# Two fp32 decoder blocks on one core: square products in 512-column chunks to the end of the row, last K tiles by token tile, and matmuls of constants at the start

## The chip, the core and the metric

The kernel runs on one core of one Trainium2 chip. The metric is the device time of one execution in microseconds, the median of several runs. TensorE (PE) multiplies; VectorE (DVE) and ScalarE (ACT) do the rest of the arithmetic; GpSimd (POOL) makes masks; SyncE's queue (SP) issues the DMAs.

## The reference

256 tokens of width 2048 go through two blocks, all in fp32. What matters here are the products of a 256-row activation with a wide weight matrix:

```python
# first block
proj = x @ w_in + b_in                     # 2048 -> 5376: conv value, glu, gate; q, k, v; gate
y_conv = layer_norm(conv31(c_val * sigmoid(c_glu))) ...   # depthwise, 31 taps
y = concat([y_conv, y_attn]) @ w_out + b_out              # square: 2048 -> 2048
x = layer_norm(ALPHA * x + y)
# second block, two layers (i = 0, 1)
y = mixer(x) @ w_out_a   (or w_out_b)                     # square
x = layer_norm(ALPHA2 * x + y)
x = x + (p[i] @ w_ple[i]) * sigmoid(x @ w_gate[i])        # square
```

So there are five square products, `w_out`, `w_out_a_2`, `w_gate0`, `w_out_b_2` and `w_gate1`. The first, second and fourth each lead into a layer norm over all 2048 columns; `w_gate1` is the last product of the kernel, and its result is stored.

## The kernel before

**Products.** TensorE takes fp32 operands here in a reduced form (`F32R`), so every operand is split into a high and a low part, and a product is three matmuls: high x high, high x low, low x high. Weights arrive by DMA as `raw`; ScalarE rounds them to `whi` (L277) and VectorE subtracts to get `wlo` (L278). `granules` (L291) walks the K tiles of a chunk of columns in groups of 128x1024 weights: two K tiles of 512 columns or four of 256. It keeps two groups cast ahead and three loaded ahead, over four buffers each of `whi` and `wlo` and six of `raw`. After each group it steps the side work by `side.pump()` (heads of the attention, the convolution's taps, rows of a norm), queued on VectorE behind the `wlo` of that group.

**`gemm`** (L315) has the activations stationary and the weights moving, for a chunk of up to 512 columns: an accumulator of two banks, one for each token tile `tt`, and for each K tile three matmuls into either bank (L324 to L326). **`gemm_T`** (L329) has the weights stationary and gives a transposed result: for each K tile a matmul of 512 moving columns for each 128 columns of weights (L336) and one of 256 (L338). The pool `acc` has two accumulators of two banks, the pool `aux` four single banks, which serve transposes, attention and the channel mean. The first product, `gv0`, has 512 columns and takes both accumulators; `total` (L341) then adds the two halves with the bias.

**Square products** run in the chunks of `SPANS` (L73):

```python
SPANS = ((0, 512), (512, 512), (1024, 512), (1536, 256), (1792, 256))
```

For `w_out` the chunks `c0` to `c4` hold eight K tiles only, as the other eight are done before. After each chunk VectorE adds it to `z` (L765, L780) and takes the statistics (`ln.stat`, L434); after the last, products of the small PLE matrices run on TensorE (`Ple.chunk`, L716; ScalarE copies each token tile's result, L720) while `ln.apply` (L436) makes mean and root, scales `z` (L448), and transposes it (L383) into scaled, shifted and split activations (L454, L459, L460). After `w_gate` ScalarE takes the sigmoid (L801), VectorE multiplies and adds (L802, L803), and the rows are stored (L805) or transposed for the next product.

**The start.** `glu(0)` runs `gv0` with the loads of x (L474) and their split (L376, L377) as events between its groups. After `kv` two transposes of `v` (L731) go to TensorE, which takes its instructions in order; the order on each engine is fixed beforehand by the framework's scheduler from estimated times.

Of the kernel before, what the change touches and what calls it, by code (L numbers as in the profile page):

```python
# [20 lines left out]
P = 128  # L21
# [9 lines left out]
LOAD = 3  # L31
PRE = 3
CONV_RATE = (3, 3)
BIG = 1e30
THETA = 10000.0

# [32 lines left out]
    **_twos("cg1", CT + 512),  # L69
}  # L70
CHUNKS_1 = {key: (ranges, ALL) for key, ranges in CHUNKS_1.items()}

SPANS = ((0, 512), (512, 512), (1024, 512), (1536, 256), (1792, 256))  # L73
CHUNKS_O1 = {
    **{f"a{c}": (_c(512 * c, 512), HIGH) for c in range(4)},
    **{f"c{c}": (_c(s, n), LOW) for c, (s, n) in enumerate(SPANS)},
# [48 lines left out]
def _cols(ranges):  # L125
    return sum(n for _, n in ranges)
# [58 lines left out]
def tile_net(ctx: ExitStack, tc: tile.TileContext, t: dict, out: bass.AP):  # L185
# [37 lines left out]
    ones_mean = const.tile([P, P], F32, name="ones_mean")  # L223
    nc.vector.memset(ones_mean, 1.0 / 1024.0)


    mask1 = const.tile([P, 384], F32, name="mask1")
    nc.gpsimd.memset(mask1, 0.0)
# [86 lines left out]
    def gemm(stream, key, act, events=None):  # L315

        n = _cols(STREAMS[stream][key][0])
        both = acc.tile([P, 2, 512], F32, tag="acc", name=uid("acc"))
        ps = [both[:, tt, :] for tt in range(2)]
        for kt, first, last, wh, wl in granules(stream, key, events):  # L320
            for tt in range(2):
                ah, al = act(kt, slice(tt * P, (tt + 1) * P))
                o = ps[tt][:, :n]
                nc.tensor.matmul(o, ah, wh, start=first, stop=False)  # L324
                nc.tensor.matmul(o, ah, wl, start=False, stop=False)  # L325
                nc.tensor.matmul(o, al, wh, start=False, stop=last)  # L326
        return [p[:, :n] for p in ps]

    def gemm_T(stream, key, act, events=None):  # L329

        nf = _cols(STREAMS[stream][key][0]) // P
        ps = [acc.tile([P, 2, 2, S], F32, tag="acc", name=uid("acc")) for _ in range(nf // 2)]
        for kt, first, last, wh, wl in granules(stream, key, events):
            both, ah = act.both(kt), act(kt, slice(0, S))[0]
            for f in range(nf):
                nc.tensor.matmul(ps[f // 2][:, f % 2], wh[:, f * P:(f + 1) * P], both, start=first, stop=False)  # L336
            for f in range(nf):
                nc.tensor.matmul(ps[f // 2][:, f % 2, 0, :], wl[:, f * P:(f + 1) * P], ah, start=False, stop=last)  # L338
        return ps

    def total(out_, ps, bias=None, scale=1.0):  # L341

        t = short((P, 2, S))
        if bias is None:
            nc.scalar.activation(t, ps[:, :, 1, :], AF.Copy, scale=scale)  # L345
        else:
            for f in range(2):
                nc.scalar.activation(t[:, f, :], ps[:, f, 1, :], AF.Identity, bias=bias1[:, bias + f:bias + f + 1])
        out_ = t if out_ is None else out_
        if scale == 1.0:  # L350
            nc.vector.tensor_tensor(out_, ps[:, :, 0, :], t, ALU.add)  # L351
        else:
            nc.vector.scalar_tensor_tensor(out_, ps[:, :, 0, :], scale, t, ALU.mult, ALU.add)
        return out_
# [373 lines left out]
    glu(2)  # L728
    glu(3)
    projected("kv", kvT)  # L730
    pt = transposes([kvT[:, 1, tt * P:(tt + 1) * P] for tt in range(2)])  # L731
    nc.scalar.copy(v1, pt[:, :S].rearrange("p (k s) -> p k s", k=2))
    for j in range(2):
        for f, h in enumerate("xy"):
            projected(f"q{j}{h}", qT[j][:, 2 * f:2 * f + 2, :])
        for i in range(4 * j, 4 * j + 4):
            side.add(attn1(i), 1, "ab"[i % 2])
        sag = unit((P, 4, S))
        for f, h in enumerate("xy"):
            projected(f"ag{j}{h}", sag[:, 2 * f:2 * f + 2, :], AF.Silu)  # L740
        sagT[j] = sag
# [424 lines left out]
```

## Time and profile before

| | us |
|---|---|
| median of 3 runs | 1449.77 |
| lowest, highest | 1449.68, 1450.47 |
| the profiled execution's own time | 1450.28 |
| its span, first to last instruction | 1448.6 |
| TensorE busy | 1432.4 (99%) |
| VectorE busy | 1032.3 (71%) |
| ScalarE busy | 802.9 (55%) |

The profile is one execution. A busy TensorE is not TensorE at its peak, as matmuls overlap: what one costs is read from start to start. In a group of instructions "xN" counts them; "[1.67 <-DVE h L351]" says that the engine had been idle for 1.67 us until line 351 on VectorE released it.

### The profile page before, as it was taken

What the parts mean: (1) busy time and instruction counts of PE and PEld (TensorE: products, weight loads), DVE (VectorE), ACT (ScalarE), POOL (GpSimd) and SP (SyncE); (2) the same over time, 40 slices, a digit from 0 to 9 for tenths busy, and PEclk for the clock granted to TensorE, in tenths of its full rate; (3) what the DMA queues carried; (4) which work ended last, traced back from release to release, by engine and by line L of the source; (5) the groups of instructions that cost most, each with busy time, mean ns of one, the idle gap of its engine ahead of it and who ended that gap; (6) DMA issues with size and microseconds to landing.
All of it is one profiled execution on the core that took longest, in us unless ns stands there. A gap on an engine that the chain in (4) does not pass through costs nothing.

```text
span 1448.6 us, 21304 instructions
## 1 busy us (share of the span) xinstructions
PE 1432.4 (99%) x8076; PEld 1240.1 (86%) x8076; DVE 1032.3 (71%) x1588; ACT 802.9 (55%) x1199; POOL 23.1 (2%) x51
## 2 busy tenths in 40 slices
PE   7999999999999999999999999999999999999998
PEld 6888888888997888888898898888888888889888
DVE  6999989998679966766758655655555555575754
ACT  6445778475545556646544545655655656554442
POOL 0000000000000000000000000100100001000000
PEclk9999999999999999999999999999999999999999
DMA  9765445556375655454764555555555555586462
GB/s 300 273 202 176 153 139 173 186 186 230 92 238 160 204 162 173 148 186 152 260 201 148 184 178 187 162 176 188 169 179 175 175 176 167 185 266 218 128 219 75
DMA packets 79798, 266.01 MB, mean 184 GB/s; under 512 B 9408, under 2 KB 10048, under 8 KB 79696
## 3 DMA queue, kind: packets, MB, share of 16 engines
q1 hardware_dynamic: 79632, 264.63, 56.5%
q8 instruction: 63, 1.03, 0.3%
q14 instruction: 39, 0.32, 0.1%
q0 software_dynamic: 64, 0.03, 0.0%
HBM read 262.53 MB, written 2.10 MB: 183 GB/s over the span
## 4 chain that ended last, share of the span: by engine, by line
PE 93%; DVE 4%; DMA 1%; issue 1%; ACT 1%; DVEq 0%; SPq 0%
PE acc L336 31%; PE acc L338 15%; PE acc L324 14%; PE acc L326 14%; PE acc L325 14%; DVE wlo L278 1%; PE o L602 1%; PE pt L383 1%; PE pT L578 1%; PE o L603 0%; DVE u L448 0%; DVE u L509 0%; PE z L1044 0%; PE z L1062 0%; DMA raw<-in_w_in_a 0%
## 5 line engine op out<-in xcount | busy, mean ns | idle before, releaser
L278 DVE TENSOR_TENSOR wlo<-raw,whi 128x1024 fp32r<-128x1024 f32 (+3 forms) x475 | 563.2, 1190 | 309.0 <-ACT whi L277 304.6
L277 ACT CAST whi<-raw 128x1024 fp32r<-128x1024 f32 (+3 forms) x475 | 485.2, 1025 | 489.3 <-PE acc L336 220.4
L336 PE MATMUL acc<-u,whi 128*128 128x512 f32 x2016 | 637.2, 399 | 7.3 <-DVE u L377 5.6
L338 PEld LDWEIGHTS acc<-u,wlo 128*128 128x128 f32 x2016 | 377.0, 188 | 87.7
L338 PE MATMUL acc<-u,wlo 128*128 128x256 f32 x2016 | 394.9, 279 | 0.0
L324 PE MATMUL acc<-whi,u 128*128 128x512 f32 (+3 forms) x1004 | 359.0, 358 | 0.0
L325 PE MATMUL acc<-wlo,u 128*128 128x512 f32 (+3 forms) x1004 | 355.9, 354 | 0.8 <-DVE wlo L278 0.8
L326 PE MATMUL acc<-whi,u 128*128 128x512 f32 (+3 forms) x1004 | 355.6, 354 | 0.0
L336 PEld LDWEIGHTS acc<-u,whi 128*128 128x128 f32 x2016 | 309.3, 189 | 14.2 <-ACT whi L277 5.6
L326 PEld LDWEIGHTS acc<-whi,u 128*128 128x128 f32 x1004 | 189.7, 189 | 25.4 <-DVE u L377 0.4
L324 PEld LDWEIGHTS acc<-whi,u 128*128 128x128 f32 x1004 | 189.8, 189 | 25.0 <-issue 1.7
L325 PEld LDWEIGHTS acc<-wlo,u 128*128 128x128 f32 x1004 | 189.9, 189 | 24.3 <-DVE wlo L278 1.2
L509 DVE SCALAR_TENSOR_TENSOR u<-u,convw,u 128x255 f32<-128x255 f32 (+19 forms) x240 | 109.2, 465 | 3.9
L351 DVE TENSOR_TENSOR h<-acc,h 128x512 f32<-128x512 f32 x51 | 34.8, 684 | 4.8 <-ACT h L345 4.8
L376 ACT CAST u<-h 128x512 fp32r<-128x512 f32 (+1 forms) x32 | 18.0, 566 | 25.3 <-DVE h L615 17.5
L466 DVE TENSOR_TENSOR u<-u,h 128x1024 f32<-128x1024 f32 x24 | 28.5, 1219 | 3.4 <-DMA h<-in_ln_g 3.3
L377 DVE TENSOR_TENSOR u<-h,u 128x512 fp32r<-128x512 f32 (+1 forms) x32 | 19.7, 622 | 14.4 <-ACT u L376 14.1
L1034 POOL TENSOR_SCALAR_AFFINE_SELECT h<-h 128x256 f32<-128x256 f32 x32 | 18.1, 564 | 743.8 <-DVE h L1054 715.7
L558 ACT ACTIVATE u<-u,negm 128x128 f32<-128x128 f32 x64 | 28.4, 445 | 2.7 <-DVE negm L550 2.6
L345 ACT ACTIVATE h<-acc 128x512 f32<-128x512 f32 x42 | 24.9, 593 | 5.5 <-PE acc L338 4.0
L802 DVE TENSOR_TENSOR h<-h,u 128x512 f32<-128x512 f32 (+1 forms) x20 | 10.8, 582 | 20.8 <-ACT h L801 20.8
L277 ACT CAST u<-raw 128x1024 fp32r<-128x1024 f32 (+1 forms) x17 | 17.3, 1015 | 14.2 <-DMA raw<-in_w_ple 7.4
(197 smaller groups left out, 962.8 us busy)
## 6 DMA issues: line engine op xcount, KB each, us to landing
raw<-in_w_in_a SPq DMA_DIRECT2D x80, 512.0 KB, 3.6
raw<-in_w_in SPq DMA_DIRECT2D x76, 512.0 KB, 3.4
raw<-in_w_gate SPq DMA_DIRECT2D x64, 512.0 KB, 3.6
raw<-in_w_kv_b SPq DMA_DIRECT2D x64, 512.0 KB, 3.4
raw<-in_w_q_b SPq DMA_DIRECT2D x64, 512.0 KB, 3.3
raw<-in_w_out SPq DMA_DIRECT2D x32, 512.0 KB, 3.4
raw<-in_w_out_a SPq DMA_DIRECT2D x32, 512.0 KB, 4.3
raw<-in_w_out_b SPq DMA_DIRECT2D x32, 512.0 KB, 4.4
```

The costliest lines, as they stand in the source:

```text
L277: nc.scalar.copy(hi, raw)
L278: return hi, lo, nc.vector.tensor_tensor(lo, raw, hi.bitcast(F32), ALU.subtract)
L324: nc.tensor.matmul(o, ah, wh, start=first, stop=False)
L325: nc.tensor.matmul(o, ah, wl, start=False, stop=False)
L326: nc.tensor.matmul(o, al, wh, start=False, stop=last)
L336: nc.tensor.matmul(ps[f // 2][:, f % 2], wh[:, f * P:(f + 1) * P], both, start=first, stop=False)
L338: nc.tensor.matmul(ps[f // 2][:, f % 2, 0, :], wl[:, f * P:(f + 1) * P], ah, start=False, stop=last)
L345: nc.scalar.activation(t, ps[:, :, 1, :], AF.Copy, scale=scale)
L351: nc.vector.tensor_tensor(out_, ps[:, :, 0, :], t, ALU.add)
L466: nc.vector.tensor_tensor(self.z[c], self.z[c], r.unsqueeze(1).broadcast_to([P, 2, 512]), op)
L509: nc.vector.scalar_tensor_tensor(o[:, d:], h[:, :S - d], w, o[:, d:], ALU.mult, ALU.add)
L558: nc.scalar.activation(sc[:, i, cs], sc[:, i, cs], AF.Exp, bias=negm[:, i, tt:tt + 1], scale=-1.0, accum_out=den[:, i, tt:tt + 1],)
```

## The change

It does five things. `SPANS` becomes four chunks of 512 columns, for all five square products. `gemm` keeps back the K tiles of a chunk's last group and then issues them by token tile: all of token tile 0, then all of token tile 1. `gemm_T` gives `gv0`, its only product with four column tiles, one accumulator and two banks of `aux`, and `total` adds such a pair bank by bank. Nine fp32 matmuls of a constant with itself go to TensorE first. And the two transposes of `v` with the copy to `v1` move from behind `kv` to behind `q0x` and `q0y`.

```diff
--- before.py
+++ after.py
@@ -31,6 +31,7 @@
 LOAD = 3
 PRE = 3
 CONV_RATE = (3, 3)
+WARM = 9
 BIG = 1e30
 THETA = 10000.0
 
@@ -69,8 +70,7 @@
     **_twos("cg1", CT + 512),
 }
 CHUNKS_1 = {key: (ranges, ALL) for key, ranges in CHUNKS_1.items()}
-
-SPANS = ((0, 512), (512, 512), (1024, 512), (1536, 256), (1792, 256))
+SPANS = tuple((512 * c, 512) for c in range(4))
 CHUNKS_O1 = {
     **{f"a{c}": (_c(512 * c, 512), HIGH) for c in range(4)},
     **{f"c{c}": (_c(s, n), LOW) for c, (s, n) in enumerate(SPANS)},
@@ -223,6 +223,10 @@
     ones_mean = const.tile([P, P], F32, name="ones_mean")
     nc.vector.memset(ones_mean, 1.0 / 1024.0)
 
+    idle = bank("idle")
+    for i in range(WARM):
+        nc.tensor.matmul(idle[:, 0:P], ones_mean, ones_mean, start=True, stop=True)
+
 
     mask1 = const.tile([P, 384], F32, name="mask1")
     nc.gpsimd.memset(mask1, 0.0)
@@ -317,36 +321,57 @@
         n = _cols(STREAMS[stream][key][0])
         both = acc.tile([P, 2, 512], F32, tag="acc", name=uid("acc"))
         ps = [both[:, tt, :] for tt in range(2)]
+
+        def product(tt, kt, first, last, wh, wl):
+            ah, al = act(kt, slice(tt * P, (tt + 1) * P))
+            o = ps[tt][:, :n]
+            nc.tensor.matmul(o, ah, wh, start=first, stop=False)
+            nc.tensor.matmul(o, ah, wl, start=False, stop=False)
+            nc.tensor.matmul(o, al, wh, start=False, stop=last)
+
+        ends = STREAMS[stream][key][1][-_group(*STREAMS[stream][key]):]
+        late = []
+        for step in granules(stream, key, events):
+            late.append(step)
+            if step[0] in ends and not step[2]:
+                continue
+            for tt in range(2):
+                for one in late:
+                    product(tt, *one)
+            late = []
+        return [p[:, :n] for p in ps]
+
+    def gemm_T(stream, key, act, events=None):
+
+
+
+
+        nf = _cols(STREAMS[stream][key][0]) // P
+        two = acc.tile([P, 2, 2, S], F32, tag="acc", name=uid("acc"))
+        ps = [two[:, f] for f in range(2)]
+        ps += [bank("acc").rearrange("p (h s) -> p h s", h=2) for _ in range(2, nf)]
         for kt, first, last, wh, wl in granules(stream, key, events):
-            for tt in range(2):
-                ah, al = act(kt, slice(tt * P, (tt + 1) * P))
-                o = ps[tt][:, :n]
-                nc.tensor.matmul(o, ah, wh, start=first, stop=False)
-                nc.tensor.matmul(o, ah, wl, start=False, stop=False)
-                nc.tensor.matmul(o, al, wh, start=False, stop=last)
-        return [p[:, :n] for p in ps]
-
-    def gemm_T(stream, key, act, events=None):
-
-        nf = _cols(STREAMS[stream][key][0]) // P
-        ps = [acc.tile([P, 2, 2, S], F32, tag="acc", name=uid("acc")) for _ in range(nf // 2)]
-        for kt, first, last, wh, wl in granules(stream, key, events):
-            both, ah = act.both(kt), act(kt, slice(0, S))[0]
+            pair, ah = act.both(kt), act(kt, slice(0, S))[0]
             for f in range(nf):
-                nc.tensor.matmul(ps[f // 2][:, f % 2], wh[:, f * P:(f + 1) * P], both, start=first, stop=False)
+                nc.tensor.matmul(ps[f], wh[:, f * P:(f + 1) * P], pair, start=first, stop=False)
             for f in range(nf):
-                nc.tensor.matmul(ps[f // 2][:, f % 2, 0, :], wl[:, f * P:(f + 1) * P], ah, start=False, stop=last)
-        return ps
+                nc.tensor.matmul(ps[f][:, 0, :], wl[:, f * P:(f + 1) * P], ah, start=False, stop=last)
+        return [two, ps[2:]][:nf // 2]
 
     def total(out_, ps, bias=None, scale=1.0):
 
         t = short((P, 2, S))
+        out_ = t if out_ is None else out_
+        if isinstance(ps, list):
+            for f, p in enumerate(ps):
+                nc.scalar.activation(t[:, f, :], p[:, 1, :], AF.Identity, bias=bias1[:, bias + f:bias + f + 1])
+                nc.vector.tensor_tensor(out_[:, f, :], p[:, 0, :], t[:, f, :], ALU.add)
+            return out_
         if bias is None:
             nc.scalar.activation(t, ps[:, :, 1, :], AF.Copy, scale=scale)
         else:
             for f in range(2):
                 nc.scalar.activation(t[:, f, :], ps[:, f, 1, :], AF.Identity, bias=bias1[:, bias + f:bias + f + 1])
-        out_ = t if out_ is None else out_
         if scale == 1.0:
             nc.vector.tensor_tensor(out_, ps[:, :, 0, :], t, ALU.add)
         else:
@@ -728,11 +753,12 @@
     glu(2)
     glu(3)
     projected("kv", kvT)
-    pt = transposes([kvT[:, 1, tt * P:(tt + 1) * P] for tt in range(2)])
-    nc.scalar.copy(v1, pt[:, :S].rearrange("p (k s) -> p k s", k=2))
     for j in range(2):
         for f, h in enumerate("xy"):
             projected(f"q{j}{h}", qT[j][:, 2 * f:2 * f + 2, :])
+        if j == 0:
+            pt = transposes([kvT[:, 1, tt * P:(tt + 1) * P] for tt in range(2)])
+            nc.scalar.copy(v1, pt[:, :S].rearrange("p (k s) -> p k s", k=2))
         for i in range(4 * j, 4 * j + 4):
             side.add(attn1(i), 1, "ab"[i % 2])
         sag = unit((P, 4, S))
```

## Rows read from the trace of the kernel before

**Rows 1.** Page, part 4: chain that ended last, shares of the span by engine.

```profile
PE 93%; DVE 4%; DMA 1%; issue 1%; ACT 1%; DVEq 0%; SPq 0%
```

**Rows 2.** Waits of TensorE, whole run: total us, times, longest us.

```profile
PE acc L336 <- DVE h L351: 1.7, 1, 1.7
PE pt L383 <- DVE h L351: 1.6, 1, 1.6
```

**Rows 3.** Windows, TensorE alone: stretch, length, busy us (count), PEclk, DMA share, GB/s.

```profile
1316.86:1339.90 23.04, 23.04 (x194) 1.00 0.58 188
1339.90:1350.81 10.91, 10.91 (x50) 1.00 0.28 96
```

**Rows 4.** Timeline, 0-34 and 303 us: start, length, engine, line, operation, tiles, count.

```profile
5.59 2.04 PE L336 MATMUL acc<-u,whi 128*128 128x512 f32 x4 [5.59 <-DVE u L377]
...
10.80 1.09 PE L336 MATMUL acc<-u,whi 128*128 128x512 f32 x4
...
25.82 0.62 ACT L376 CAST u<-h 128x512 fp32r<-128x512 f32 x1 [2.05 <-DMA h<-in_xT]
...
26.47 0.69 DVE L377 TENSOR_TENSOR u<-h,u 128x512 fp32r<-128x512 f32 x1 [1.98 <-ACT u L376]
...
27.64 1.09 PE L336 MATMUL acc<-u,whi 128*128 128x512 f32 x4
...
27.95 3.67 DVE L278 TENSOR_TENSOR wlo<-raw,whi 128x1024 fp32r<-128x1024 f32 x3
...
29.97 0.63 PE L338 MATMUL acc<-u,wlo 128*128 128x256 f32 x4
...
32.27 0.73 PE L336 MATMUL acc<-u,whi 128*128 128x512 f32 x2 [1.67 <-DVE h L351]
...
303.00 0.70 PE L647 MATMUL cm<-u,ones_mean 128*128 128x256 f32 x2
```

**Rows 5.** Windows: length; busy us of PE, PEld, DVE, ACT, POOL; PEclk, DMA share.

```profile
15.00:20.00 5.00, 5.00 (x30) 4.33 (x29) 3.09 (x6) 2.89 (x6) 0.00 (x0) 1.00 1.00 320
...
40.00:60.00 20.00, 20.00 (x116) 17.45 (x116) 19.75 (x34) 9.48 (x12) 0.00 (x0) 1.00 0.78 273
```

**Rows 6.** Timeline, 113 to 116 us: around the transposes of `v`.

```profile
113.20 0.63 PE L336 MATMUL acc<-u,whi 128*128 128x512 f32 x2
...
114.65 0.68 DVE L351 TENSOR_TENSOR h<-acc,h 128x512 f32<-128x512 f32 x1
...
115.48 0.41 PE L383 MATMUL pt<-ident,h 128*128 128x128 f32 x2 [1.65 <-DVE h L351]
```

**Rows 7.** Timeline, 62 to 67 us: one group's low half and its first use.

```profile
62.92 1.22 DVE L278 TENSOR_TENSOR wlo<-raw,whi 128x1024 fp32r<-128x1024 f32 x1
...
66.29 0.40 PE L338 MATMUL acc<-u,wlo 128*128 128x256 f32 x2
```

**Rows 8.** Timeline, 763 to 770 us: end of `w_out_a_2`, VectorE and ScalarE.

```profile
763.94 0.76 DVE L780 SCALAR_TENSOR_TENSOR u<-u,acc 128x256 f32<-128x256 f32 x2 [0.58 <-PE acc L326]
...
766.68 1.08 ACT L720 COPY u<-acc 128x512 f32<-128x512 f32 x2 [1.69 <-PE acc L326]
...
769.40 1.07 ACT L720 COPY u<-acc 128x512 f32<-128x512 f32 x2 [1.22 <-PE acc L326]
```

**Rows 9.** Timeline, two chunks' ends of `w_gate1`; stores: count, KB, us to landing.

```profile
1420.47 1.09 ACT L801 ACTIVATE h<-acc 128x512 f32<-128x512 f32 x2 [1.67 <-PE acc L326]
...
1423.02 0.95 SPq L805 DMA_DIRECT2D out<-u  x2
...
1443.50 0.66 ACT L801 ACTIVATE h<-acc 128x256 f32<-128x256 f32 x2 [9.92 <-PE acc L326]
...
1445.04 0.81 SPq L805 DMA_DIRECT2D out<-u  x2
...
out<-u SPq DMA_DIRECT2D x6, 256.0 KB, 2.2
...
out<-u SPq DMA_DIRECT2D x4, 128.0 KB, 1.9
```

## Prediction, made before the changed kernel ran

> **What bounds the kernel now.** I read the chain of work that ended last first: TensorE holds 93% of it [rows 1], so a microsecond of TensorE work or of TensorE waiting is a microsecond of the kernel, apart from what lies after its last matmul. Then the table of who waited for whom, for TensorE: two long waits on VectorE besides the first one, 1.7 us in the product `g1` and 1.6 us in a transpose [rows 2]. Then the stretches in which only one kind of matmul runs, for the price of a matmul from start to start [rows 3]; the "mean ns of one" of a group is a latency and cannot be used, because matmuls overlap. Last, the timelines at the start, at 113 us, at the end of a square product and at the end of the kernel [rows 4, 6, 8, 9].
>
> **The change, part by part.**
>
> *Chunks of 512.* Each of the five square products ends in two chunks of 256 columns, now in one of 512. A 256-column matmul costs 23.04 us / 192 = 120.0 ns (the stretch counts 194 because it touches one on either side), a 512-column one 10.91 / 48 = 227.3 ns [rows 3]. So two halves cost 12.7 ns more than the whole: something of about 13 ns is paid per matmul, whatever its width. A chunk is 16 K tiles x 2 token tiles x 3 = 96 matmuls, 48 where the product has eight K tiles: 4 x 192 + 96 = 864 of 256 columns go, 432 of 512 take their place: 864 x 0.1200 - 432 x 0.2273 = 103.7 - 98.2 = **-5.5 us**, all on the path, since these stretches show TensorE busy without a gap. Weight loads, casts and groups of weights (128x1024 each, eight for the last 512 columns either way) keep their sizes and number. The Trainium skill, "TensorE: Matmul & The Clock Gate", section "Back-to-back issue gap", has 2.5 ns per matmul beside N/2.4: by that page the part would be worth 432 x 2.5 = 1.1 us (an estimate from the page), and the whole change 4.4 us less than below; the rows' 120.0 and 227.3 ns, against its 109 and 216, disagree with it, and the measurement decides.
>
> *Two more banks for `gv0`.* The first product has held both accumulator tiles, so `g1` could not start before VectorE had read one: TensorE's last matmul of `gv0` starts at 30.32 (the fourth of the 29.97 row), the next at 32.27 [rows 4]. With the other half of `gv0` in two auxiliary banks, `g1` has a free tile. Its first weights are there: the low halves of its first three groups, one of which lasts TensorE 2.8 us, are made from 27.95 to 31.62. Start to start 1.95 us less the 0.12 of one matmul: **-1.8 us**. The two added VectorE adds are half as wide; they cost VectorE some 0.15 us and TensorE nothing. The auxiliary banks are next asked for at 115 us [rows 6].
>
> *Transposes of `v` after `q0x`, `q0y`.* TensorE's row of matmuls stops at 113.43 (the second of the 113.20 row) and goes on with a transpose at 115.48, which waits for VectorE's total of `kv` at 114.65 [rows 6]. That total is late because VectorE is late, not TensorE. Behind 22 us of `q0` matmuls the total is long done: 2.04 - 0.23 = **-1.8 us**. What moves along is a bank and ScalarE's copy to `v1`, behind the casts and totals of `q0`; nothing on SP or POOL. `v1` is first used by a head's last matmuls, after its softmax, which itself comes after `q0`.
>
> *Nine warm-up matmuls.* TensorE is idle until 5.59 us [rows 4]. No row shows such a matmul at that hour. The nearest is the 256-column fp32 matmul of `channel_mean`, 0.70 us in work at full clock with its two records [rows 4]: nine of them are 6.3 us, would end at some 7.4 and hold up the first product by 1.8; from below the price is nothing. With half the columns, at half the clock, overlapping, I take 3 us, hidden in the idle time. What they may give: the first four wide matmuls take 2.04 us and later ones 1.09 [rows 4], the spacing of 1.2 and of 2.4 GHz. Two K tiles take from 5.59 to 10.80, the next twelve from there to 27.64, 1.40 each; at full clock the first two would save 5.21 - 2.80 = 2.4 us. But the product cannot end sooner than its data: the last pair of x tiles lands at 25.8, is split by 27.16, and its matmuls start at 27.64 [rows 4], while the DMA engines are busy throughout [rows 5]. So at most 27.64 - 27.16 = 0.48 arrives: **-0.4 us** (bounds 0 and -2.4, the latter if loads come sooner too).
>
> *Is VectorE able to follow?* From 40 to 60 us it is busy 19.75 of 20 us [rows 5], so its results come no sooner when TensorE does. The tightest group of weights has its low half done at 62.92 + 1.22 = 64.14 and is first used at 66.29 [rows 7]: 2.15 us of slack, against 1.8 + 0.4 = 2.2 gained before it. Here 0.0 to 0.3 us comes back: **+0.2 us**. I found no tighter group in the first 140 us.
>
> *Last K tiles by token tile.* Would token tile 0 be read sooner? The rows speak against it: VectorE's two adds after a chunk start together at 763.94, after 0.58 us of waiting, though token tile 0 was complete 0.36 us before the last matmul; ScalarE's copies at 766.68 likewise [rows 8]. Both token tiles lie in one tile of two banks, and the first reader waits for its last matmul. So **0**.
>
> *The longer end of a chunk.* With 512 columns in the last chunk and no earlier release, what follows gets longer. At the kernel's end a 512-column chunk takes from 1420.47 to the end of its second store's issue at 1423.97 = 3.50 us, a 256-column one from 1443.50 to 1445.85 = 2.35; stores of 256 KB take 0.3 us longer to land (2.2 against 1.9) [rows 9]: **+1.45 us**, all on the path, since TensorE is done. At the three norms adds and statistics take 0.8 to 1.5 us longer (up to twice 0.76 for each of the two pairs [rows 8]); there PLE matmuls run (24 x 0.2273 = 5.5 us, twice that at the last), and the first scaling on ScalarE stands behind the copies at 769.40 + 1.07 anyway [rows 8]. That hides it but for some 0.1 us each: **+0.25** (bounds 0 and 1.8).
>
> Sum: -5.5 - 1.8 - 1.8 - 0.4 + 0.2 + 1.45 + 0.25 = **-7.6 us**. Against the profiled execution's own 1450.28 that is 1442.7; that execution lies 0.5 above the median of the three runs, 1449.77, so I forecast **1442.2** for a median.
>
> **Rivals.**
>
> *Early release.* If the new program does let token tile 0 be read when its own six last matmuls are done, 1.36 us before the end, half of each pair of copies leaves the path (0.5 us at three norms [rows 8]), and the kernel's tail shrinks to about that of 256 columns (-1.15), and the +0.25 goes: -10.5, 1439.3. For it: the reorder makes the lead four times what it was. Against: the 0.58 us that VectorE waited. The Trainium skill, "PSUM — Partial Sum Buffer", section "Summary: rules for kernel authors", lets another bank be read while a matmul runs, so the chip would allow it; no run here shows it yet.
>
> *VectorE takes the front back.* If the order in VectorE's queue turns out worse than the slack above, TensorE waits for low halves of weights between 40 and 140 us, and the 1.8 + 1.8 + 0.4 come back less the 0.2 already counted: -7.6 + 3.8 = -3.8, 1446.0. For it: 19.75 of 20 us [rows 5]. Against: 2.15 us of slack in the tightest group [rows 7]. Counted with it, at 0.02 of its 0.13, is the case that a matmul's fixed price is not what the rows show: if only a fifth of the 12.7 ns went with each of the 432, 1.1 us of the 5.5 would be left, 1446.6. Against: both spacings held over 192 and 48 matmuls [rows 3]. (That fifth is about what the page named above gives.)
>
> *Slower.* The order on each engine is laid down beforehand from estimated times, and changes with every edit. A transpose placed before its data costs TensorE 1.8 us, as at 113 us. The transposes of 16 heads and the norm's 8 groups all wait for a VectorE that runs late. From 6 such stops on (6 x 1.8 = 10.8 > 7.6 + 2.9) the kernel is slower by over 0.2%; with 7, 1449.8 - 7.6 + 12.6 = 1454.8. Against: before, one such place, that of `v`, stalls for long.
>
> *The part doesn't act.* The warm-up may leave the clock as it was: 0.4 us, inside the range.
>
> **How the numbers follow.** Forecast 0.63, its own range 1440.2 (loads come sooner) to 1443.8 (the norms' tails show); early release 0.20; VectorE takes it back 0.13; slower 0.04. 1438.7 to 1444.8 holds the forecast, most of early release and little else, about 8 in 10. A measurement of this kernel tells 0.2%, 2.9 us, from no change: faster means below 1446.9. That holds for the first two cases and for most of the third (0.91 in all); 0.05 within; 0.04 slower.
>
> **What would show it.** Right: on the three lines of `gemm` 432 matmuls fewer and none of 256 columns; the last product's end some 9 us earlier than 1443.5; no wait of `g1` or of the `v` transposes; both adds after a chunk still starting together; a tail about 1.4 us longer. Wrong: matmuls of 512 columns spaced over 230 ns in the last chunk, waits on `wlo` in the first 140 us, the second reader of a chunk starting 1.36 us after the first, or new stops at transposes.

## The result, and the profile after

The changed kernel takes 1441.71 us, median of 6 runs (1440.68 to 1443.9), against 1449.72 of the kernel before (1448.77 to 1453.32): a ratio of 0.9942, 95% interval 0.993 to 0.9955, or 8.0 us less. The forecast was 1442.2 in a range of 1438.7 to 1444.8. The two profiled executions are further apart, 1450.28 and 1441.06, since one lies 0.6 above its median and the other 0.7 below. Their spans, 1448.58 and 1439.31, differ by 9.27 us, and that is what the table takes apart. A step is the change in the start of one stage of TensorE against the stage before it.

| part | forecast | profiles, after less before |
|---|---|---|
| wait of `g1` for an accumulator | -1.8 | -1.83 |
| rest of the first product (clock) | -0.4 | -0.21 |
| a low half of weights that comes late, at 72 us | +0.2 | +0.26 |
| transposes of `v` | -1.8 | -1.92 |
| five square products with their norms, to the last matmul | -5.5 + 0.25 | -5.87 |
| one stop at 462 us | not foreseen | -0.92 |
| from the last matmul to the end | +1.45 | +1.17 |
| other steps | | +0.05 |
| sum | -7.6 | -9.27 |

First the chain of waits of the changed kernel, as shares of the span. Before, VectorE held 4% of it [rows 1]; now TensorE has all but a few per cent.

```profile
PE 97%; DVE 1%; ACT 0%; DMA 0%; issue 0%; SPq 0%; DVEq 0%
```

The waits of TensorE (total, times, longest) answer [rows 2]: the two long ones are gone, and what is left stands at the start (L228 is the constant's first matmul, L402 splits x, L356 multiplies) and at the norms (L473 scales, L408 transposes).

```profile
PE acc L356 <- DVE u L402: 1.6, 4, 0.7
PE idle L228 <- DVE halfpi L878: 1.2, 1, 1.2
PE pt L408 <- DVE u L473: 0.5, 1, 0.5
PE pt L408 <- ACT h L479: 0.3, 1, 0.3
```

The timeline of TensorE at the places of [rows 4] and [rows 6]. The constant's matmuls run from 1.15 to 5.36 us and the first four wide matmuls take 1.17 instead of 2.04; at 9.54 TensorE waits for x, as it did not before. `g1` starts at 30.23, straight behind `gv0`. At 72.03 two wide matmuls are followed after 0.74 us, not 0.47. The transposes of `v`, at 130.94, wait for nothing.

```profile
1.15 4.21 PE L228 MATMUL idle<-ones_mean 128*128 128x128 f32 x18 [1.15 <-DVE halfpi L878]
5.78 1.17 PE L356 MATMUL acc<-u,whi 128*128 128x512 f32 x4 [0.42 <-DVE u L402]
...
9.54 1.21 PE L356 MATMUL acc<-u,whi 128*128 128x512 f32 x4 [0.73 <-DVE u L402]
...
29.75 0.64 PE L358 MATMUL acc<-u,wlo 128*128 128x256 f32 x4
30.23 0.63 PE L356 MATMUL acc<-u,whi 128*128 128x512 f32 x2
...
72.03 0.63 PE L356 MATMUL acc<-u,whi 128*128 128x512 f32 x2
72.77 0.51 PE L358 MATMUL acc<-u,wlo 128*128 128x256 f32 x2
...
130.94 0.38 PE L408 MATMUL pt<-ident,h 128*128 128x128 f32 x2
```

A window over the last product's last chunk, TensorE alone: 48 matmuls and one touched on either side in 10.91 us, as before in a chunk of 512 columns [rows 3].

```profile
1421.50:1432.41 10.91, 10.91 (x50) 1.00 0.00 0
```

Last, a chunk's end in `w_out_a_2` and the kernel's end, as in [rows 8, 9]. Both readers of an accumulator still stand in one row, and only the first of them waited for TensorE. The first sigmoid (L827) starts after the last matmul's end at 1433.02, and the second store's issue ends at 1436.54.

```profile
757.36 1.29 DVE L806 SCALAR_TENSOR_TENSOR u<-u,acc 128x512 f32<-128x512 f32 x2 [0.41 <-PE acc L330]
...
1433.06 1.08 ACT L827 ACTIVATE h<-acc 128x512 f32<-128x512 f32 x2 [9.82 <-PE acc L330]
1433.69 1.29 DVE L828 TENSOR_TENSOR h<-h,u 128x512 f32<-128x512 f32 x2 [9.20 <-ACT h L827]
1434.90 1.29 DVE L829 TENSOR_TENSOR u<-u,h 128x512 f32<-128x512 f32 x2
1435.61 0.93 SPq L831 DMA_DIRECT2D out<-u  x2
```

### The profile page after: what moved, and what is told of

Read it like the earlier page. It is cut to its first block, busy times and chain, and to the rows that moved or that the text cites. A ratio compares the mean times of both kernels' runs of the same rounds, so it can differ in the third digit from the quotient of the medians.

```text
span 1439.3 us, 20447 instructions
## 1 busy us (share of the span) xinstructions
PE 1429.0 (99%) x7662; PEld 1220.4 (85%) x7662; DVE 1029.5 (72%) x1569; ACT 803.6 (56%) x1195; POOL 23.1 (2%) x51
## 4 chain that ended last, share of the span: by engine, by line
PE 97%; DVE 1%; ACT 0%; DMA 0%; issue 0%; SPq 0%; DVEq 0%
PE acc L356 32%; PE acc L358 16%; PE acc L328 14%; PE acc L330 14%; PE acc L329 14%; PE pt L408 1%; PE o L627 1%; PE pT L603 1%; PE o L628 0%; PE z L1070 0%; PE z L1088 0%; PE s L570 0%; DMA h<-in_xT 0%; DVE wlo L282 0%; PE o L618 0%; PE s L568 0%
## 5 line engine op out<-in xcount | busy, mean ns | idle before, releaser
L282 DVE TENSOR_TENSOR wlo<-raw,whi 128x1024 fp32r<-128x1024 f32 (+3 forms) x475 | 563.6, 1191 | 314.0 <-ACT whi L281 309.5
L356 PE MATMUL acc<-u,whi 128*128 128x512 f32 x2016 | 636.5, 398 | 1.6 <-DVE u L402 1.6
L328 PE MATMUL acc<-whi,u 128*128 128x512 f32 (+2 forms) x860 | 334.1, 388 | 0.0
L329 PE MATMUL acc<-wlo,u 128*128 128x512 f32 (+2 forms) x860 | 330.6, 384 | 0.0
L330 PE MATMUL acc<-whi,u 128*128 128x512 f32 (+2 forms) x860 | 330.5, 384 | 0.0
L356 PEld LDWEIGHTS acc<-u,whi 128*128 128x128 f32 x2016 | 308.3, 189 | 9.1 <-issue 5.0
L330 PEld LDWEIGHTS acc<-whi,u 128*128 128x128 f32 x860 | 161.6, 188 | 30.8 <-DVE u L402 0.4
L328 PEld LDWEIGHTS acc<-whi,u 128*128 128x128 f32 x860 | 161.6, 188 | 30.5 <-issue 1.7
L329 PEld LDWEIGHTS acc<-wlo,u 128*128 128x128 f32 x860 | 161.8, 188 | 28.6 <-DVE wlo L282 0.2
L534 DVE SCALAR_TENSOR_TENSOR u<-u,convw,u 128x255 f32<-128x255 f32 (+22 forms) x240 | 108.0, 466 | 3.3
L401 ACT CAST u<-h 128x512 fp32r<-128x512 f32 (+1 forms) x32 | 18.0, 566 | 22.0 <-DVE h L640 18.8
L402 DVE TENSOR_TENSOR u<-h,u 128x512 fp32r<-128x512 f32 (+1 forms) x32 | 19.7, 622 | 10.2 <-ACT u L401 10.0
L828 DVE TENSOR_TENSOR h<-h,u 128x512 f32<-128x512 f32 x16 | 10.4, 689 | 19.1 <-ACT h L827 19.1
```

The source lines that it names most:

```text
L282: return hi, lo, nc.vector.tensor_tensor(lo, raw, hi.bitcast(F32), ALU.subtract)
L356: nc.tensor.matmul(ps[f], wh[:, f * P:(f + 1) * P], pair, start=first, stop=False)
L534: nc.vector.scalar_tensor_tensor(o[:, d:], h[:, :S - d], w, o[:, d:], ALU.mult, ALU.add)
```

## The experiments

The theory: the parts add up; the square products gain a fixed price per matmul; the order by token tile gives nothing because both token tiles lie in one tile; the clock gives next to nothing because x has to land. The rivals: the price per matmul is smaller, the order releases something, VectorE takes the front back. In the expectations "the page" with its 2.5 ns is the page of the Trainium skill that the prediction names for the price of a matmul. The runs come in four groups, each with runs of the kernel before beside it: the three single parts and "token tiles apart" in the first, where "before" was 1449.71; the four from "the kernel before once more" to "eight chunks" in the second, 1449.95; the version in turn, the four K tiles and the halves in the third, 1451.25; the last version in the fourth, 1451.17. So "before" itself moved by 1.5 us between groups, and where two versions come from different groups, a median proves no difference of a microsecond: there the stages of the profiles are compared.

### One part alone: the chunks

```diff
-SPANS = ((0, 512), (512, 512), (1024, 512), (1536, 256), (1792, 256))
+SPANS = tuple((512 * c, 512) for c in range(4))
```

> The kernel before with SPANS as four chunks of 512 columns and nothing else. Theory (a fixed price of some 12.7 ns per matmul): 432 pairs of 256-column matmuls become 432 of 512, -5.5 us up to the last product's end, +1.2 us of longer work behind the last matmul, so about -4 us (1445.5); last matmul's end about 5.5 us earlier than 1443.5. Rival (the page's 2.5 ns per matmul): -1.1 up to the last matmul, so about +0.1 in all. A second question: the 0.8 us for which TensorE waited on VectorE's low halves of weights near 462 us, and which is gone in the changed kernel. If it is gone here, the new chunks in the first square product reordered VectorE's queue there, and the run gives -5; if it stays, it belongs to one of the other parts.

Measured: 1445.33, -4.4 us, ratio 0.9971 (0.996 to 0.9982). The profiled execution, 1443.85, is the fastest of the seven, and that of before lies 0.6 above its median, so the two profiles differ by 6.5 us; what follows compares their stages. The last matmul ends 7.6 us earlier than before, at 1435.82, of which 0.9 is the stop at 462, which is gone here, and 0.7 lies before `w_out` (two stops that vary, see below). From the first matmul of `w_out` to the last of PLE behind it TensorE takes 93.67 us instead of 94.37, for `w_out_a_2` 94.69 instead of 95.99, for `w_gate0` 92.03 instead of 93.82, for `w_out_b_2` to `w_gate1` 191.37 instead of 194.05. The theory's matmuls alone make -0.61, -1.22, -1.22 and -2.44. The excess of 0.57 in `w_gate0` is two stops at transposes between the matmuls of its halves, which now stand behind the product: the next stretch is 0.51 longer. The other three exceed the theory by 0.08 to 0.24. A price of 2.5 ns would have left the time where it was; that rival falls.

### One part alone: the banks of `gv0`

```diff
-        ps = [acc.tile([P, 2, 2, S], F32, tag="acc", name=uid("acc")) for _ in range(nf // 2)]
+        two = acc.tile([P, 2, 2, S], F32, tag="acc", name=uid("acc"))
+        ps = [two[:, f] for f in range(2)]
+        ps += [bank("acc").rearrange("p (h s) -> p h s", h=2) for _ in range(2, nf)]
...
```

> The kernel before with the first product's second half in two auxiliary banks and nothing else. Theory: the first matmul of g1 follows the last of gv0 without the 1.67 us wait, -1.8 us at g1, and at most 0.3 us of it is given back between 40 and 140 us: -1.6 us (1448.1). Rival (VectorE takes the front back): g1 starts 1.8 us sooner, but the start of w_out is no more than 0.3 us sooner. The wait near 462 us is here as before, unless a shift of the front by 1.8 us alone removes it.

Measured: 1446.41, -3.3 us, ratio 0.9978 (0.9969 to 0.9987); twice what was expected. The wait of `g1` is gone. Against the second profile of before (below) the steps are -1.8 at `g1`, +0.7 at 72 us, where TensorE waits for a low half of weights, and -0.8 at the stop at 462: together -1.8. Against the first profile there are 0.7 more at the start and 0.55 at the transposes of `v`, but by these the two profiles of before differ from one another as well. So the edit accounts for 1.8 us in the profiles; why the median moved by 3.3 stays open.

### One part alone: the transposes of `v`

```diff
     projected("kv", kvT)
-    pt = transposes([kvT[:, 1, tt * P:(tt + 1) * P] for tt in range(2)])
-    nc.scalar.copy(v1, pt[:, :S].rearrange("p (k s) -> p k s", k=2))
     for j in range(2):
         for f, h in enumerate("xy"):
             projected(f"q{j}{h}", qT[j][:, 2 * f:2 * f + 2, :])
+        if j == 0:
+            pt = transposes([kvT[:, 1, tt * P:(tt + 1) * P] for tt in range(2)])
+            nc.scalar.copy(v1, pt[:, :S].rearrange("p (k s) -> p k s", k=2))
```

> The kernel before with the two transposes of v and the copy to v1 moved behind q0x and q0y, and nothing else. Theory: the 1.65 us wait of the transpose goes and nothing else waits instead: start of ag0x 1.8 to 1.9 us sooner, the same at w_out, -1.8 us in all (1447.9). Rival (the stop moves): the transposes wait in their new place, or a head's last matmuls wait for v1, and less than 0.5 us is left at w_out.

Measured: 1448.1, -1.6 us, ratio 0.999 (0.9982 to 0.9999). The start of `ag0x` against that of `q0x` is 1.93 us sooner than in the profiled execution of before, and 0.10 of it is gone at `w_out`. Nothing waits in the new place. The stop itself varies: TensorE waited 1.65 us there in the first profile of before [rows 6], 1.2 in the run of the chunks alone and 1.1 in a second profile of before, against which the move is worth 1.3. The stop at 462 us is gone here too. With it that makes 2.2 us, more than the median's 1.6, but within its interval, 0.1 to 2.6.

### The kernel before once more: the stop at 462 us

> The kernel before, unchanged, for a second profiled execution: is TensorE's 0.8 us wait on VectorE's low halves of weights near 462 us part of the program, or of that one execution? If of the program, it stands here too, at the same place, with 0.7 to 1.0 us, and each of the three single edits removed it by shifting the work; if of the execution, it is absent or of another size, and the 0.9 us have no place in a comparison of medians.

The wait is there again, by the timeline, with 0.74 us (0.76 in the first profile). So it is not of the first execution alone. VectorE is late there: one of its products with the norm's gain (L466) waited 2.74 us for a row that the DMA brought.

```profile
443.66 1.22 DVE L466 TENSOR_TENSOR u<-u,h 128x1024 f32<-128x1024 f32 x1 [2.74 <-DMA h<-in_ln_g]
...
462.26 0.50 PE L325 MATMUL acc<-wlo,u 128*128 128x512 f32 x1 [0.74 <-DVE wlo L278]
```

With the transposes of `v` moved and nothing else, that wait is a fifth as long (the row of the bias costs 0.52 more), and TensorE does not stop:

```profile
440.56 1.22 DVE L466 TENSOR_TENSOR u<-u,h 128x1024 f32<-128x1024 f32 x1 [0.54 <-DMA h<-in_ln_g]
```

The stop stands in both profiles of before, where that product waited 1.81 and 2.74 us; no other kernel of this study, the three with a single part included, has one of over 0.3 us there. That the edits took it away is not shown: in the other twelve profiles the wait for the row is 0.41 to 1.87 us, and the two with the longest, 1.87 and 1.85, stop TensorE for some 0.2 us there. If each part alone removes it, each is credited with its 0.9 us: the three sum to -4.4 - 3.3 - 1.6 = -9.3, less twice 0.9 is -7.5, beside the -8.0 of the whole. Each of the three is uncertain by more than 1 us either way, so this agreement says little. Why the row lands later in the kernel before was not settled; its issue stands behind seven loads of weights in the same queue with the stop and without.

### The changed kernel without the constant's matmuls

```diff
-    idle = bank("idle")
-    for i in range(WARM):
-        nc.tensor.matmul(idle[:, 0:P], ones_mean, ones_mean, start=True, stop=True)
```

> The changed kernel without the nine matmuls of the constant at its start. Theory: the first four wide matmuls are at half the clock again (2.04 instead of 1.17 us), the clock rises near 10.7 us, but the last matmuls of gv0 wait for the last x pair all the same: g1 starts 0.2 to 0.5 us later than in the changed kernel, and the time is 1441.7 + 0.3 = 1442.0, which five rounds can hardly tell from no change. Rival (loads follow TensorE, so that a faster start also brings x sooner): +2 us, 1443.7.

Measured: 1442.13 (1440.54 to 1442.26) beside 1441.71: no difference that could be told. In the profiles `g1` starts at 30.44 instead of 30.23, but the late low half at 72 us is not there, so that `kv` starts at 97.32 instead of 97.49. The loss at `g1` is 0.2 us, the gain at 72 us 0.4.

### The changed kernel without the order by token tile

```diff
-        ends = STREAMS[stream][key][1][-_group(*STREAMS[stream][key]):]
-        late = []
-        for step in granules(stream, key, events):
-            ...
+        for kt, first, last, wh, wl in granules(stream, key, events):
+            for tt in range(2):
+                ...
```

> The changed kernel with the last K tiles of a chunk in their old order, token tile 0 and 1 in turn for each K tile. Theory: nothing is lost, since both token tiles lie in one tile and its first reader waits for the last matmul in either order: 1441.7 within 0.5, with both readers starting together and the last matmul to the last store's issue 3.5 us as before. Rival (the order released something): up to +1.4 us, 1443.1.

Measured: 1441.06 (1440.67 to 1442.77). The profiles lie on one another: last matmul's end 1433.02 in both, span 1439.30 and 1439.31, first sigmoid at 1433.05 and 1433.06. Without the order TensorE is 0.2 us later at `g1` and gains as much between 440 and 510 us; at the norms and the end nothing differs. As it stands in the change, the order is worth nothing.

### Eight chunks of 256 columns

```diff
-SPANS = tuple((512 * c, 512) for c in range(4))
+SPANS = tuple((256 * c, 256) for c in range(8))
```

> The changed kernel with eight chunks of 256 columns in all five square products. 1728 matmuls of 512 columns become 3456 of 256. Theory (12.7 ns paid per matmul whatever its width): +21.9 us, less 1.15 of shorter work behind the last matmul: 1441.7 + 20.8 = 1462.5; spacing 120.0 ns throughout. Rival (the page's 2.5 ns per matmul): +4.3 - 1.15, 1444.9. If VectorE cannot follow twice as many adds and statistics, more than 1463 and waits on its low halves of weights.

Measured: 1465.49, 23.8 us above the changed kernel where 20.8 was expected, and 3.2 at 2.5 ns per matmul. The stretch of `w_out_b_2`, which has no added stop, is 4.88 us longer: 384 added matmuls times 12.7 ns is 4.88. The window over 192 matmuls (and three touched) of `w_gate1` has the 120.0 ns of [rows 3]:

```profile
1366.00:1389.04 23.04, 23.04 (x195) 1.00 0.46 134
```

The 3 us more are stops: 1.3 us in three places in `w_out` at 309 to 313 us, where split activations come late twice and a low half of weights once, and a stop of 0.2 to 0.3 us at each of seven transposes between the chunks of `w_gate0`. The Trainium skill, "TensorE: Matmul & The Clock Gate", section "Back-to-back issue gap", puts the price beside the columns at 2.5 ns for the gap of a matmul by itself; in the rows of matmuls of this kernel it is 12.7.

### Token tiles apart

The last chunk of each square product and all PLE chunks get a tile of their own for token tile 1.

```diff
         ps = [both[:, tt, :] for tt in range(2)]
+        if apart:
+            ps[1] = bank("acc")
...
+        ps = gemm("w_out", f"c{c}", y1, apart=c == NB - 1)
```

> The changed kernel, with token tile 1 of the last chunk of each square product, and of every PLE chunk, in an auxiliary bank: two tiles where there was one tile of two banks. Theory (a reader waits for the last matmul into its tile, and the order by token tile released nothing because both token tiles shared a tile): now the first reader of such a chunk starts about 1.36 us before its last matmul, the second after it; the work behind the last matmul shrinks from 3.5 to about 2.2 us, and the PLE copies start sooner by 1.3 us. That gives -1.2 to -1.5 us against the changed kernel (1440.3). Rival (the chip or the scheduler holds the first reader back until the product is complete, or VectorE is busy elsewhere): both readers still start together, and the time is the changed kernel's, 1441.7.

Measured: 1438.17 (1438.12 to 1438.39), ratio to before 0.9924 (0.9911 to 0.9936), 3.5 us less than the changed kernel and 2.9 by the profiles; more than expected. The timeline of the kernel's end:

```profile
1429.93 0.60 ACT L829 ACTIVATE h<-acc 128x512 f32<-128x512 f32 x1 [8.46 <-PE acc L332]
...
1430.56 0.69 DVE L830 TENSOR_TENSOR h<-h,u 128x512 f32<-128x512 f32 x1 [7.84 <-ACT h L829]
...
1431.28 0.69 DVE L831 TENSOR_TENSOR u<-u,h 128x512 f32<-128x512 f32 x1
1431.29 0.60 ACT L829 ACTIVATE h<-acc 128x512 f32<-128x512 f32 x1 [0.76 <-PE acc L332]
1431.92 0.69 DVE L830 TENSOR_TENSOR h<-h,u 128x512 f32<-128x512 f32 x1
1432.00 1.69 SPq L833 DMA_DIRECT2D out<-u  x2
1432.64 0.69 DVE L831 TENSOR_TENSOR u<-u,h 128x512 f32<-128x512 f32 x1
```

The two sigmoids are rows of their own now, each waits for TensorE, and the first starts 1.36 us before the second, while TensorE is still at work. That is what the changed kernel lacked, and it shows that a reader may take one bank while matmuls write another; so has it the Trainium skill, "PSUM — Partial Sum Buffer", section "Summary: rules for kernel authors". From the last matmul's end to the span's end it is 5.12 us instead of 6.29. At the three norms, which the expectation had left out, TensorE gains 0.47 us (`w_out`), 0.59 (`w_out_a_2`) and 0.29 (`w_out_b_2`). That makes 2.5 of the 2.9 us; the other 0.4 lie at the start and between 440 and 510 us, places that this edit does not touch. The same pair of versions without the constant's matmuls (the first experiment on the changed kernel and the last below) gives 0.45, 0.59 and 0.31 at the norms and again 1.17 at the end. So by stages the edit is worth 2.5 us; the further microsecond of the medians is in no profile: the six runs of the changed kernel spread over 3.2 us, the five of this version over 0.3. TensorE's waits at transposes (0.5 and 0.3 in the list above) are gone:

```profile
PE idle L228 <- DVE halfpi L880: 1.2, 1, 1.2
PE acc L358 <- DVE u L404: 1.0, 4, 0.3
PE acc L330 <- DVE u L486: 0.3, 1, 0.3
```

### Token tiles apart, K tiles in turn

The edit of "without the order" on the version with token tiles apart.

> The version with token tiles apart in the last chunks, but with the K tiles in their old order (token tiles in turn). Theory (the order is worth something only once the tiles are apart): token tile 0 is complete three matmuls, 0.68 us, before the last instead of six, 1.36; at the kernel's end VectorE's four passes of 0.65 us then start 0.68 later and follow one another without a gap, so the tail grows by about 0.5 us, and the norms by 0.1 each: 1438.2 + 0.8 = 1439.0. Rival (separate tiles alone do it): 1438.2.

Measured: 1439.08 (1439.0 to 1439.36), 0.9 us more than with the order, where 0.8 was expected; but the two come from groups whose "before" lies 1.5 us apart, and the ratios to before are the same (0.9921 and 0.9924), so the stages decide. The tail is 5.67 us instead of 5.12, because VectorE's four passes now follow one another:

```profile
1431.30 1.28 ACT L819 ACTIVATE h<-acc 128x512 f32<-128x512 f32 x2 [9.14 <-PE acc L333]
...
1431.93 1.37 DVE L820 TENSOR_TENSOR h<-h,u 128x512 f32<-128x512 f32 x2 [8.52 <-ACT h L819]
1433.22 1.28 DVE L821 TENSOR_TENSOR u<-u,h 128x512 f32<-128x512 f32 x2
1433.93 0.94 SPq L823 DMA_DIRECT2D out<-u  x2
```

At the norms the order changes nothing (0.05, 0.03 and -0.01 us, where 0.1 each was expected). The rest of the 1.24 us between the two profiles is 0.2 at the start and 0.5 between 440 and 510 us, which the version with halves below, which keeps the order, has as well. So the order is worth 0 with one tile and 0.55 us with two, all of it behind the last matmul. The second tile alone is worth 2.0 us: against the changed kernel without the order, 0.43, 0.59 and 0.33 at the norms and 0.62 behind the last matmul.

### Four K tiles by token tile, and a last chunk in halves

```diff
-        ends = STREAMS[stream][key][1][-_group(*STREAMS[stream][key]):]
+        ends = STREAMS[stream][key][1][-_group(*STREAMS[stream][key]) * (2 if apart else 1):]
```

> The version with token tiles apart, with the last two groups of weights (four K tiles) of those chunks by token tile instead of one: token tile 0 is complete 2.7 us before the last matmul. Theory: at the end nothing is gained, since token tile 1's sigmoid, product, sum and store bind and do not wait for token tile 0; at the norms 0 to 0.2 us each: 1437.9 within 0.4. Rival (weights held longer starve the casts, which have four buffers): waits of TensorE on whi or wlo at the ends of chunks, 1439 or more.

```diff
-                sg = short((P, n))
-                zz = z[q][:, tt, at:at + n]
+                m = n // 2 if final and c == NB - 1 and tt else n
+                for b in range(0, n, m):
+                    sg = short((P, m))
+                    zz = z[q][:, tt, at + b:at + b + m]
...
```

> The version with token tiles apart, with token tile 1 of the very last chunk read, added and stored in two halves of 256 columns. Theory: the chain sigmoid 0.60, product 0.69, sum 0.69 of token tile 1 becomes 0.35 and then four passes of about 0.37 on VectorE: the last sum ends 0.1 to 0.2 us sooner, and a store of 128 KB lands some 0.2 sooner than one of 256: 1437.9. Rival (each pass, and each store's issue on SP, has a fixed price that eats it): 1438.2 or more.

Measured: 1439.25 (1438.52 to 1440.59) and 1438.49 (1438.06 to 1440.08): no gain in either that could be told. In the first the tail is 5.11 us against 5.12; no wait on weights shows, so the rival of starved casts isn't there. In the second it is 5.03, 0.09 less, where 0.3 to 0.4 had been hoped for: four passes of 256 columns on VectorE take 0.75 + 0.75 us, two of 512 took 0.69 + 0.69, and three stores instead of two are issued. Both profiles lie 1.2 to 1.3 us behind at `g1` (31.34 and 31.26 against 30.03), although the constant's matmuls ran; here is the start in the first of them:

```profile
1.16 4.21 PE L228 MATMUL idle<-ones_mean 128*128 128x128 f32 x18 [1.16 <-DVE halfpi L880]
6.03 2.05 PE L358 MATMUL acc<-u,whi 128*128 128x512 f32 x4 [0.66 <-DVE u L404]
```

The first wide matmuls are at the spacing of 1.2 GHz again, as without the constant's matmuls.

### Token tiles apart, without the constant's matmuls

> The version with token tiles apart, without the nine matmuls of the constant at the start. Theory (the last x pair binds the first product, and its landing varies by a microsecond between executions): g1 starts between 29.7 and 30.5 us although the first two K tiles run at half the clock, and the time is that of the version with them, 1438.2 within 0.5. Rival (the matmuls of the constant are worth the 0.4 us of the forecast or more): g1 at 30.6 or later and 1438.6 to 1439.5.

Measured: 1438.37 (1437.63 to 1439.2) against 1438.17 with them, from another group: no difference that could be told. The profile is the shortest of all, a span of 1435.88 us. `g1` starts at 29.77, though the first K tile ran at the spacing of half the clock (2.69 us; later ones take 1.40), and the late low half at 72 us is missing. On VectorE that low half (L279 here) is put before part of the work that is queued ahead of it when the constant's matmuls are there (L282 in the changed kernel, next fence):

```profile
67.33 1.59 DVE L533 SCALAR_TENSOR_TENSOR u<-u,convw,u 128x227 f32<-128x227 f32 x4
68.83 0.69 DVE L717 SCALAR_TENSOR_TENSOR u<-u,h 128x512 f32<-128x512 f32 x1
69.44 0.47 DVE L533 SCALAR_TENSOR_TENSOR u<-u,convw,u 128x249 f32<-128x249 f32 x1
69.83 0.69 DVE L717 SCALAR_TENSOR_TENSOR u<-u,h 128x512 f32<-128x512 f32 x1
70.43 1.22 DVE L279 TENSOR_TENSOR wlo<-raw,whi 128x1024 fp32r<-128x1024 f32 x1
```

```profile
67.66 2.71 DVE L534 SCALAR_TENSOR_TENSOR u<-u,convw,u 128x229 f32<-128x229 f32 x7
70.29 1.28 DVE L718 SCALAR_TENSOR_TENSOR u<-u,h 128x512 f32<-128x512 f32 x2
71.49 1.22 DVE L282 TENSOR_TENSOR wlo<-raw,whi 128x1024 fp32r<-128x1024 f32 x1
```

Seven taps of the convolution and both adds (L718) stand ahead, behind the last total, instead of five taps and both adds (L717): from that total's start to the low half's it is 4.43 us instead of 3.70. All versions with the constant's matmuls have the pause at 72 us, of 0.27 to 0.29 us, whether `g1` started at 29.95 or at 31.34.

## Why the prediction was right, step by step

*Chunks.* Right, by its own reason. The 12.7 ns per matmul that were worked out of [rows 3] held for 432 matmuls fewer (-5.5 of -5.9) and for 1728 more (21.9, and stops on top). Two more widths in the changed kernel fit. Its windows from the first start to the 124th at 384 columns, and from the first to the 47th at 336 (two touched ones are counted along), give 21.32 / 123 = 173 ns and 7.03 / 46 = 153: about 0.419 ns per column and 12.7 beside them, at all four widths. In the two windows of [rows 3] TensorE counts 193 and 49 weight loads beside the 194 and 50 matmuls: the 12.7 ns are the price of a matmul with its own load, and no run parts the two.

```profile
365.00:386.32 21.32, 21.32 (x124) 1.00 0.29 90
405.78:412.81 7.03, 7.03 (x49) 1.00 0.81 287
```

*Norms.* Small, and smaller than forecast: +0.25 for the three, measured -0.09, +0.17 and -0.07 us beside the theory of the chunks, from each product's start to behind its norm. The adds and statistics mostly stayed hidden behind PLE's matmuls; only at `w_out_a_2` do TensorE's transposes wait, 0.5 us for the scaling (L473 in the list above).

*Banks and transposes of `v`.* Right: -1.83 and -1.92 in these profiles. Both are waits whose length changes from one execution to the next (1.6 to 1.8 for `g1`, 1.1 to 1.65 for `v`); the two figures came from one execution, and against the second profile of before they come to 1.7 and 1.3.

*VectorE's slack.* Right in size for the changed kernel (+0.26 at 72 us), wrong in reason, and it was another group. It was to be the group used at 66.29 us, with its 2.15 us of slack against 2.2 us gained. The late low half is that of the third group after it, which before was done 3.1 us ahead of its first use:

```profile
70.35 1.22 DVE L278 TENSOR_TENSOR wlo<-raw,whi 128x1024 fp32r<-128x1024 f32 x1
...
74.65 0.40 PE L338 MATMUL acc<-u,wlo 128*128 128x256 f32 x2
```

What changed is the order in VectorE's queue: before, one tap stood between the last total and this low half; with the banks alone, or all but the constant's matmuls, five taps and both adds; with the constant's matmuls seven and both adds, whenever TensorE started. With the banks alone 0.7 us was lost there, so the margin is thin in either of the new orders.

*Clock.* The -0.4 failed. The step that failed is "the product cannot end sooner than its data", put at the last pair of x: what binds comes earlier. With the clock up, TensorE stops for x at 9.54, 12.89 and 16.12 us (0.73, 0.27 and 0.17), and runs without a stop from there on; at half the clock it comes too late to wait as long. The last of the three stops is no late load. That pair had landed at 13.39; ScalarE cast it (L401) at 14.65, behind a cast of weights that had waited 1.30 us for TensorE:

```profile
14.12 0.62 ACT L281 CAST whi<-raw 128x512 fp32r<-128x512 f32 x1 [1.30 <-PE acc L356]
...
14.65 0.62 ACT L401 CAST u<-h 128x512 fp32r<-128x512 f32 x1
```

In all seven profiles with the constant's matmuls one more cast of weights stands ahead of this pair's than in the seven without them, and it is cast 1.2 to 2.0 us after it has landed, there within 0.6; from this stop to `g1` it is 14.1 us in all seven. So the matmuls of the constant also come with another order on ScalarE, which holds back the start that they were to speed up. What that alone costs was not measured. The landings vary as well, that of the second pair between 7.61 and 8.65 us in the same seven. With the banks and without the constant's matmuls `g1` started at 29.70, 29.77 and 30.44; with them at 29.95, 30.03, 30.22, 30.23, 30.37, 31.26 and 31.34. The nine matmuls took 4.2 us, not the 3 assumed, still in idle time.

*Order by token tile.* Right, 0, and for the reason given: with a tile for each token tile the reader starts 1.36 us sooner. The rival "early release" was priced at 2.9 us below the forecast's sum: 1.5 at the norms, 1.15 at the end, and the 0.25 that goes. The version that makes its condition true gains 1.35 and 1.17 by stages; the 0.25 was not there to go. Its mechanism and its price were nearly right; that the change doesn't fulfil its condition spoke against it.

*Tail.* Forecast +1.45, measured +1.17. The work behind the last matmul grew from 2.35 to 3.48 us, as forecast (1.15). The mis-sized term is the landing: 0.3 us more was taken from medians over stores of both sizes, [rows 9]; at the kernel's end it was 0.04, from 2.73 to 2.77 us.

*The stop at 462 us.* Not foreseen. It stood in the list of waits of before with 0.8 us, and the prediction left it out.

*The sum.* That the medians' -8.0 came so near to the -7.6 is in part luck. Stage by stage the two profiles differ by 9.27 us, 1.7 beyond the sum: 0.9 of it is the stop at 462, 0.6 the products with their norms, 0.3 the tail. The medians differ by less because one profile lay 0.6 above its median and the other 0.7 below.

## What to carry to other kernels

Give each independent reader's part of an accumulator its own tile: here both token tiles in one tile made a reorder of matmuls worthless, and apart the same reorder and the tile gave 2.5 us by stages (3.5 by the medians), 2.0 of them without the reorder, so that the version of 1438.17 us beats both kernels. Read the price of a matmul from start to start at two widths; the difference of 2 x 120.0 and 227.3 ns foretold the matmuls' part of both runs with other chunk widths; the stops that came with 256 columns, 3 us, it did not. A single-part run in a kernel whose queues are laid down beforehand can also lose a stop that has nothing to do with its part, so sums of single parts can exceed the whole; compare stages as well as totals. And an edit on one engine can change the order on another: look for that before a time is put down to the edit itself.

## What the runs showed of the hardware

TensorE's clock at the start did not always follow the constant's matmuls. Of seven profiles with them, the first four wide matmuls took 1.17 to 1.20 us in four, 1.54 in one, and 2.04 and 2.05, the spacing of 1.2 GHz, in two. In these two TensorE had gone on with the first product at 6.03 and 6.04 us, in the others between 5.56 and 5.78. The column of granted clock reads 1.00 in all these stretches, so the level is read from the spacing alone.

And the moment at which the first product ends is not the program's alone: in two executions of the kernel before, `g1` started at 32.27 and at 31.43 us. In the changed versions it started between 29.70 and 31.34 us in ten profiles of kernels that do the same work there, with and without the constant's matmuls, and so with two orders on ScalarE. That is 1.6 us, about as much as the move of the transposes is worth.
